# Gate, branch and output projections of a hybrid encoder block with the tokens stationary, and transposes behind them

## The chip, the cores and the metric

The kernel runs on one core of one Trainium2 chip. The metric is the device time of one execution in microseconds (us), the median of several runs; lower is better. The core's engines are TensorE (PE for its matmuls, PEld for its weight loads), VectorE (DVE), ScalarE (ACT), GpSimd (POOL) and SyncE (SP), which here issues most DMAs.

## The reference

One encoder layer over 256 tokens of width 2048, in float32. What matters here is the part between the input projection and the gated MLP:

```python
proj = jnp.einsum('bld,de->ble', rms_norm(x, g_mix[layer]), w_in[layer])   # 10240 columns
q, k, v, hy, gates = jnp.split(proj, splits, axis=-1)                       # gates: 2 x 2048
a_branch = jnp.einsum('ble,ed->bld', att.reshape(b, l, V_COLS), w_attn_branch[layer])   # 1024 -> 2048
h_branch = jnp.einsum('blc,cd->bld', y_hy, w_hyena_branch[layer])                       # 1024 -> 2048
g_a, g_h = jnp.split(gates, 2, axis=-1)
merged = jax.nn.sigmoid(g_a) * a_branch + jax.nn.sigmoid(g_h) * h_branch
x = x + jnp.einsum('bld,de->ble', merged, w_out[layer])                                 # 2048 -> 2048
hf = rms_norm(x, g_ffn[layer])
up = dwconv3(jnp.einsum('bld,df->blf', hf, w_up[layer]), ...)                           # 2048 -> 11264
x = x + jnp.einsum('blf,fd->bld', jax.nn.silu(gate_u) * val_u, w_down[layer])           # 5632 -> 2048
return rms_norm(x, g_final)
```

## The kernel before, in words

All weights are streamed once, in **chunks** of 128x1024 numbers (512 KB): two row blocks (k-tiles) of 128 rows by 512 columns. A chunk is loaded into `wr` (five buffers), and split into a high part `wh` (ACT cast) and a low part `wl` (DVE subtraction), three buffers each, so that two fp32r operands stand for one float32. Activations are split in the same way: an operand tile holds, for each k-tile, 256 columns of the high part and 256 of the low part, side by side. The product of the two low parts is left out.

A **group** is 512 output columns of one weight matrix, over all its k-tiles. `add_group` puts the group's chunks into one list; the main loop goes over that list (`for i in range(n)`, line 891): it issues the load of chunk i+5, the split of chunk i+2 and the matmuls of chunk i, then takes one finished step of an earlier group (`flush(1)`) and some of the background work (`run_bg`: filter, long convolution, attention heads). The framework's scheduler then sets each engine's order from that; an engine runs its own instructions strictly in that order. The groups come as hyena projections (6), gate h (4, `w_in` 16 to 19), v (2), branch h (4, `w_hb`), q and k (4), gate a (4, `w_in` 12 to 15), branch a (4, `w_ab`), output (4, `w_out`), up (22, `w_up`) and down.

`emit_mm` knows two forms for one k-tile:

- **channel-major** (`toks=None`): weights stationary. For each of four blocks of 128 output channels, one matmul of `wh` with 512 moving columns (both parts of the 256 tokens) and one of `wl` with 256. That is 8 matmuls and 4 x 768 = 3072 moving columns a k-tile, a *pair* for each block. The result lies with channels on partitions, in four PSUM banks, each with two halves that still have to be added (`merged_sum`: ACT copies one half, DVE adds the other).
- **token-major** (`toks=(0, 1)`): tokens stationary, the weight moving. For each of two blocks of 128 tokens, three matmuls of 512 moving columns (x high with `wh`, x high with `wl`, x low with `wh`). That is 6 matmuls and 2 x 3 x 512 = 3072 moving columns a k-tile, a *triple* for each block. The result lies with tokens on partitions, in two banks, and is complete.

Before the change, v and down are token-major, and everything else is channel-major. A gate's step (4 a group) is `merged_sum`, a multiplication by `rstd` and a sigmoid; for gate a the sigmoids are kept back (`gate_gen`) until attention has ended. Branch a's step merges both branches and splits the sum into `mg`, the operand of the output projection. The output projection's step adds the residual `x2T` (reloaded from `xT` in DRAM by `reload_x`), writes the scaled split of the sum into `xg`, the operand of up, and sums the squares for the norm; after the last group `norm` makes `rstd` from a matmul with ones (`rs2_ps`). Since down wants the residual with tokens on partitions, `x2tok_gen` then transposes `x2T` on TensorE, 8 times 4 transposes into `xt_ps`, among the first chunks of up.

Of the kernel before, what the change touches and what calls it, by code (L numbers as in the profile page):

```python
# [11 lines left out]
F32 = mybir.dt.float32  # L12
# [34 lines left out]
def block(ctx: ExitStack, tc: tile.TileContext, a, out):  # L47
# [20 lines left out]
    def add(o, x, y):  # L68
        tt(o, x, y, ALU.add)
# [4 lines left out]
    def mul(o, x, y):  # L74
        tt(o, x, y, ALU.mult)
# [10 lines left out]
    def act(o, x, f, **kw):  # L86
        nc.scalar.activation(out=o, in_=x, func=f, **kw)  # L87
# [99 lines left out]
    def merged_sum(pt, name):  # L187
        lo = etile("lo", f"lo_{name}")
        nc.scalar.copy(out=lo, in_=pt[:, T:])  # L189
        s = etile("sum", f"s_{name}")  # L190
        add(s, pt[:, :T], lo)
        return s
# [54 lines left out]
    def xop(kk):  # L247
        return xg[kk // 4][:, kk % 4, :]

    # ------------------------------------------------------------------ hyena  # L250
    hy = {}

    def hy_groups():
# [173 lines left out]
                split(yhy[ct // 4][:, ct % 4, :T], yhy[ct // 4][:, ct % 4, T:], z)  # L427
                yield

    # ------------------------------------------------------------------ gates and branches  # L430
    mix = {}

    def gate_h_groups():
        def step(g, c):
            def f(pts):
                if g == 0 and c == 0:
                    mix["h"] = [s8(f"mh{i}", [P, 8, T]) for i in range(2)]
                ct = g * 4 + c
                s = merged_sum(pts[c], f"gh{ct}")
                mul(s, s, rstd)  # L440
                act(mix["h"][ct // 8][:, ct % 8, :], s, AF.Sigmoid)
            return f
        for g in range(4):
            add_group(a["w_in"][16 + g], KT, 512, xop, [step(g, c) for c in range(4)])

    def branch_h_groups():
        def step(g, c):
            def f(pts):
                ct = g * 4 + c
                s = merged_sum(pts[c], f"bh{ct}")  # L450
                m = mix["h"][ct // 8][:, ct % 8, :]
                mul(m, m, s)
            return f
        for g in range(4):
            add_group(a["w_hb"][g], 8, 512, lambda kk: hy["y"][kk // 4][:, kk % 4, :],
                      [step(g, c) for c in range(4)])

    def gate_a_group(g):
        def step(c):
            def f(pts):  # L460
                if g % 2 == 0 and c == 0:
                    mix["ga", g // 2] = s8(f"ga{g // 2}", [P, 8, T])
# [4 lines left out]
        add_group(a["w_in"][12 + g], KT, 512, xop, [step(c) for c in range(4)])  # L467

    def gate_gen():
        for t in range(16):  # L470
            o = mix["ga", t // 8][:, t % 8, :]
            with tc.issue_after(at["end"]):
                act(o, o, AF.Sigmoid)
            if t % 4 == 3:
                yield

    def branch_a_group(g):
        def step(c):
            def f(pts):
                if g == 0 and c == 0:  # L480
                    mix["m"] = [s8(f"mg{i}", [P, 4, 512], F32R) for i in range(4)]
                ct = g * 4 + c
# [6 lines left out]
        add_group(a["w_ab"][g], 8, 512, lambda kk: at["o"][kk // 4][:, kk % 4, :], [step(c) for c in range(4)])  # L489

    # ------------------------------------------------------------------ attention
    at = {}

    def v_groups():
# [168 lines left out]
            stt(dst[:, h % 4, T:], pt[:, :T], at["gs"], hi.bitcast(F32), ALU.mult, ALU.subtract)  # L663
        yield

    # ------------------------------------------------------------------ output projection and FFN
    ff = {}

    def reload_x():
        ff["x2T"] = [s8(f"x2T{i}", [P, 8, T]) for i in range(2)]  # L670
        for i in range(2):
            nc.sync.dma_start(out=ff["x2T"][i], in_=a["xT"][8 * i:8 * i + 8].rearrange("k p t -> p k t"))

    def out_groups():
        def step(g, c):
            def f(pts):
                ct = g * 4 + c
                s = merged_sum(pts[c], f"wo{ct}")
                x2 = ff["x2T"][ct // 8][:, ct % 8, :]
                add(x2, x2, s)  # L680
                split_scaled(x2, ct, C_GFFN)
                sq = etile("cv", f"sq2{ct}")
                act(sq, x2, AF.Square)
                acc = sqacc[:, 0, :]
                if ct == 0:
                    nc.vector.tensor_copy(out=acc, in_=sq)
                else:
# [9 lines left out]
        def nop(pts):  # L697
            pass
        for g in range(4):
            add_group(a["w_out"][g], KT, 512, lambda kk: mix["m"][kk // 4][:, kk % 4, :],  # L700
                      [step(g, c) for c in range(4)] + ([nop, norm] if g == 3 else []))

    def x2tok_gen():
        ff["x"] = [s8(f"x2tok{t}", [P, D]) for t in range(2)]
        for t in range(2):
            for k4 in range(4):
                pt = bank(f"xt_ps{t}{k4}")
                for c in range(4):
                    kk = k4 * 4 + c
                    nc.tensor.transpose(out=pt[:, c * P:(c + 1) * P],  # L710
                                        in_=ff["x2T"][kk // 8][:, kk % 8, t * P:(t + 1) * P], identity=ident)
                nc.scalar.copy(out=ff["x"][t][:, k4 * 512:(k4 + 1) * 512], in_=pt)
                yield

    def up_groups():
        ff["m"] = {}
# [249 lines left out]

def _host(inp):
    i = {k: np.asarray(v) for k, v in inp.items()}
    r = dict(_consts())
    r["xT"] = i["x"][0].T.reshape(KT, P, T)  # L970
    order = []
    for g in range(4):
        order += [g, 4 + g]
# [53 lines left out]
```

## Time and profile before

| | |
|---|---|
| time, median of 3 runs (lowest to highest) | 1455.68 us (1455.35 to 1455.88) |
| span of the profiled execution | 1453.7 us |
| TensorE matmuls: busy, share of the span, count | 1440.7 us, 99%, 8068 |
| VectorE: busy, share | 1039.8 us, 72% |
| ScalarE: busy, share | 807.8 us, 56% |
| DMA, mean busy share of the 16 engines in 40 slices of the span | 0.3 to 0.7 |

The span runs from the first to the last instruction; the 2.0 us that the median is longer lie around it. A busy time is the union of the durations of an engine's instructions. Matmuls follow each other before the one ahead has ended, so the durations printed (0.39 us for 512 columns) overlap, and what a matmul costs is read from the distance between two starts.

### The profile page before, as it was taken

How to read it: one execution, taken by the hardware profiler on the slowest of the kernel's cores; microseconds unless marked ns; L12 is line 12 of the kernel's file. 1: busy time of each engine (PE TensorE's matmuls, PEld its weight loads, DVE VectorE, ACT ScalarE, POOL GpSimd, SP SyncE). 2: the span in 40 equal slices, each digit the busy share in tenths (PEclk: the TensorE clock that was granted, in tenths of full speed). 3: DMA queues.
4: the chain of work that ended last, by engine and by line, in shares of the span. 5: the costliest groups of instructions: out<-in, count | busy, mean ns of one | idle time of the engine just before them, and what ended most of it. 6: DMA issues, size and time to landing. Idle time of an engine off the chain costs nothing.

```text
span 1453.7 us, 21399 instructions
## 1 busy us (share of the span) xinstructions
PE 1440.7 (99%) x8068; PEld 1245.2 (86%) x8068; DVE 1039.8 (72%) x1697; ACT 807.8 (56%) x1274; POOL 13.0 (1%) x17
## 2 busy tenths in 40 slices
PE   8999999999999999999999999999999999999997
PEld 7888888888888888888888888888888888888897
DVE  7988887856677777967776786777877776545464
ACT  7655554544566656656665565555655555434353
POOL 3000000000000000000000000000000000000000
PEclk9999999999999999999999999999999999999999
DMA  7754444465544445565545555555555556555573
GB/s 274 246 174 160 164 170 170 152 234 185 175 159 146 151 144 185 197 237 190 188 171 189 182 184 188 188 189 188 181 186 187 185 189 219 196 193 192 197 253 126
DMA packets 79663, 271.96 MB, mean 187 GB/s; under 512 B 8959, under 2 KB 14112, under 8 KB 79304
## 3 DMA queue, kind: packets, MB, share of 16 engines
q1 hardware_dynamic: 78840, 269.54, 53.9%
q8 instruction: 63, 1.03, 0.3%
q10 hardware_dynamic: 720, 1.07, 0.2%
q14 instruction: 40, 0.33, 0.1%
HBM read 268.45 MB, written 2.11 MB: 186 GB/s over the span
## 4 chain that ended last, share of the span: by engine, by line
PE 97%; DVE 1%; DMA 1%; ACT 1%; issue 0%; SPq 0%; ACTq 0%; DVEq 0%
PE acc L90 93%; PE s_ps L90 1%; DMA wr<-in_w_in_dram 1%; DVE wl L66 1%; PE o_ps L90 0%; PE h_ps L90 0%; PE k_ps L90 0%; PE y_ps L90 0%; ACT wh L99 0%; PE wt_ps L611 0%; PE xt_ps L710 0%; PE ua_ps L90 0%; PE ub_ps L90 0%; DVE xg L78 0%; PE f_ps L90 0%
## 5 line engine op out<-in xcount | busy, mean ns | idle before, releaser
L90 PE MATMUL acc<-xg,wh 128*128 128x512 f32 x2560 | 908.5, 400 | 0.6 <-ACT sq L87 0.3
L66 DVE TENSOR_TENSOR wl<-wr,wh 128x1024 fp32r<-128x1024 f32 (+1 forms) x495 | 601.1, 1215 | 355.7 <-ACT wh L99 354.3
L99 ACT CAST wh<-wr 128x1024 fp32r<-128x1024 f32 (+1 forms) x495 | 516.4, 1043 | 525.7 <-PE acc L90 470.0
L90 PE MATMUL acc<-xg,wl 128*128 128x256 f32 x2560 | 716.1, 281 | 2.5 <-DVE wl L66 2.4
L90 PEld LDWEIGHTS acc<-xg,wh 128*128 128x128 f32 x2560 | 480.7, 188 | 118.6 <-issue 0.7
L90 PEld LDWEIGHTS acc<-xg,wl 128*128 128x128 f32 x2560 | 483.1, 189 | 6.1 <-DVE wl L66 4.7
L90 PE MATMUL acc<-wh,m 128*128 128x512 f32 (+1 forms) x832 | 218.2, 350 | 0.0
L90 PEld LDWEIGHTS acc<-wh,m 128*128 128x128 f32 x832 | 146.9, 189 | 20.6
L90 PE MATMUL acc<-wl,m 128*128 128x512 f32 (+1 forms) x416 | 145.7, 350 | 0.0
L90 PE MATMUL acc<-mg,wh 128*128 128x512 f32 x256 | 88.8, 391 | 0.0
L90 PEld LDWEIGHTS acc<-wl,m 128*128 128x128 f32 x416 | 78.7, 189 | 10.4 <-DVE wl L66 0.2
L90 PE MATMUL acc<-mg,wl 128*128 128x256 f32 x256 | 71.7, 280 | 0.0
L90 PEld LDWEIGHTS acc<-mg,wh 128*128 128x128 f32 x256 | 47.9, 187 | 10.5
L90 PEld LDWEIGHTS acc<-mg,wl 128*128 128x128 f32 x256 | 48.4, 189 | 0.0
L90 PE MATMUL acc<-yhy,wh 128*128 128x512 f32 x128 | 45.3, 399 | 0.0
L90 PE MATMUL acc<-att,wh 128*128 128x512 f32 x128 | 44.5, 392 | 0.0
L90 PE MATMUL acc<-wh,xg 128*128 128x512 f32 x128 | 40.5, 392 | 0.0
L78 DVE SCALAR_TENSOR_TENSOR sg<-s_up,pk,sg 128x255 f32<-128x255 f32 x88 | 39.4, 478 | 0.7
L78 DVE SCALAR_TENSOR_TENSOR vv<-s_up,pk,vv 128x255 f32<-128x255 f32 x88 | 39.3, 478 | 0.4
L189 ACT COPY lo_up<-acc 128x256 f32<-128x256 f32 x88 | 32.2, 366 | 11.5 <-PE acc L90 11.3
L90 PE MATMUL acc<-yhy,wl 128*128 128x256 f32 x128 | 35.9, 281 | 0.0
L90 PE MATMUL acc<-att,wl 128*128 128x256 f32 x128 | 35.8, 280 | 0.0
(198 smaller groups left out, 1070.8 us busy)
## 6 DMA issues: line engine op xcount, KB each, us to landing
wr<-in_w_up_dram SPq DMA_DIRECT2D x176, 512.0 KB, 3.2
wr<-in_w_in_dram SPq DMA_DIRECT2D x156, 512.0 KB, 3.3
wr<-in_w_down_dram SPq DMA_DIRECT2D x66, 512.0 KB, 3.3
wr<-in_w_out_dram SPq DMA_DIRECT2D x32, 512.0 KB, 3.3
wr<-in_w_down_t_dram SPq DMA_DIRECT2D x28, 512.0 KB, 3.9
wr<-in_w_hb_dram SPq DMA_DIRECT2D x16, 512.0 KB, 4.3
wr<-in_w_ab_dram SPq DMA_DIRECT2D x16, 512.0 KB, 3.3
wr<-in_w_in_dram SPq DMA_DIRECT2D x8, 256.0 KB, 4.4
```

The source lines that it names most:

```text
L66: nc.vector.tensor_tensor(out=o, in0=x, in1=y, op=op)
L78: nc.vector.scalar_tensor_tensor(out=o, in0=x, scalar=s, in1=y, op0=op0, op1=op1)
L90: nc.tensor.matmul(o, lhsT=lhsT, rhs=rhs, start=start, stop=stop)
L99: nc.scalar.copy(out=hi, in_=x)
L189: nc.scalar.copy(out=lo, in_=pt[:, T:])
```

## The change

- Gate h, branch h, gate a, branch a and the output projection go from channel-major to token-major (`toks=(0, 1)`); each group has two steps of 512 columns instead of four of 256, and no `merged_sum`. Gates are scaled by `rstd_tok`, a per-partition scale of the activation.
- Branch a's merged sum lies in `ga` with tokens on partitions; two further steps a group (`turn_step`) transpose it, 4 transposes a step, and split it into `mg`. The output projection does the same: the residual sum `xtok` is transposed 4 blocks a step, and `split_scaled` writes `xg` from PSUM.
- The residual `x` is loaded token-major, at the start of branch a, not at the start of the output projection; it stays in place until the end, and `x2tok_gen` is gone.
- The norm after the output projection is worked out per token (two values a partition), put on a diagonal and spread over partitions by one matmul of the same shape as before.

```diff
     def gate_h_groups():
-                s = merged_sum(pts[c], f"gh{ct}")
-                mul(s, s, rstd)
-                act(mix["h"][ct // 8][:, ct % 8, :], s, AF.Sigmoid)
+                act(mix["h"][t][:, g * 512:(g + 1) * 512], pts[t], AF.Sigmoid, scale=rstd_tok[:, t:t + 1])
-            add_group(a["w_in"][16 + g], KT, 512, xop, [step(g, c) for c in range(4)])
+            add_group(a["w_in"][16 + g], KT, 512, xop, [step(g, t) for t in range(2)], toks=(0, 1))
...
     def branch_h_groups():
-                s = merged_sum(pts[c], f"bh{ct}")
-                m = mix["h"][ct // 8][:, ct % 8, :]
-                mul(m, m, s)
+                m = mix["h"][t][:, g * 512:(g + 1) * 512]
+                mul(m, pts[t], m)
...
     def gate_a_group(g):
-                s = merged_sum(pts[c], f"ga{g}{c}")
-                o = mix["ga", g // 2][:, (g % 2) * 4 + c, :]
-                mul(o, s, rstd)
+                act(mix["ga"][t][:, g * 512:(g + 1) * 512], pts[t], AF.Copy, scale=rstd_tok[:, t:t + 1])
...
+    def to_channels(src, g, half, name):
+        pt = bank(name)
+        for j in range(2):
+            ct = g * 4 + half * 2 + j
+            for t in range(2):
+                nc.tensor.transpose(out=pt[:, j * T + t * P:j * T + (t + 1) * P],
+                                    in_=src[t][:, ct * P:(ct + 1) * P], identity=ident)
+        return pt
...
     def branch_a_group(g):
-                s = merged_sum(pts[c], f"ba{ct}")
-                mul(s, s, mix["ga", g // 2][:, (g % 2) * 4 + c, :])
-                add(s, s, mix["h"][ct // 8][:, ct % 8, :])
-                dst = mix["m"][ct // 4]
-                split(dst[:, ct % 4, :T], dst[:, ct % 4, T:], s)
+                o = mix["ga"][t][:, cs]
+                mul(o, pts[t], o)
+                add(o, o, mix["h"][t][:, cs])
+        def turn_step(half):
+            def f(pts):
+                pt = to_channels(mix["ga"], g, half, f"mt{g}{half}").rearrange("p (c t) -> p c t", c=2)
+                dst = mix["m"][g][:, half * 2:half * 2 + 2, :]
+                split(dst[:, :, :T], dst[:, :, T:], pt)
+            return f
+                  [step(0), step(1), turn_step(0), turn_step(1)], toks=(0, 1))
...
-    def reload_x():
-            nc.sync.dma_start(out=ff["x2T"][i], in_=a["xT"][8 * i:8 * i + 8].rearrange("k p t -> p k t"))
+    def load_x():
+            nc.sync.dma_start(out=ff["x"][t], in_=a["x"][t * P:(t + 1) * P, :])
     def out_groups():
-                s = merged_sum(pts[c], f"wo{ct}")
-                add(x2, x2, s)
-                split_scaled(x2, ct, C_GFFN)
-                act(sq, x2, AF.Square)
-                    add(acc, acc, sq)
+                add(x2, pts[t], x2)
+                act(sq, x2, AF.Square, accum_out=ss2[:, t, g:g + 1])
+        def turn_step(g, half):
+            def f(pts):
+                pt = to_channels(ff["x"], g, half, f"xt{g}{half}")
+                for j in range(2):
+                    split_scaled(pt[:, j * T:(j + 1) * T], g * 4 + half * 2 + j, C_GFFN)
+            return f
         def norm(pts):
-            mm(pt[:, :T], ones, sqacc[:, 0, :], True, True)
-            rsqrt_chain(rstd, pt[:, :T], T, "x2")
-            bg.append(x2tok_gen())
+            nc.vector.tensor_reduce(out=ms, in_=ss2, axis=AX.X, op=ALU.add)
...
+            for t in range(2):
+                ts(d[:, t * P:(t + 1) * P], ident, r2[:, t, 2:3], None, ALU.mult)
+            mm(pt[:, :T], ones, d, True, True)
+            nc.scalar.copy(out=rstd, in_=pt[:, :T])
-                      [step(g, c) for c in range(4)] + ([nop, norm] if g == 3 else []))
+                      [step(g, 0), step(g, 1), turn_step(g, 0), turn_step(g, 1)] + ([norm] if g == 3 else []),
+                      toks=(0, 1))
-    def x2tok_gen():
...
-    before(lambda: (drain(), setp(False, 1.0), bg.append(gate_gen())))
+    before(lambda: (drain(), setp(False, 1.0), bg.append(gate_gen()), load_x()))
-    before(reload_x)
```

Where the instructions stand. First TensorE at the start of the output projection, before the change (`acc196_0` to `_3` are the four banks of the group that starts with chunk 196, `mg0` its operand, `wh196` and `wl196` the chunk's parts):

```order
L90 MATMUL acc196_0_6245<-mg0_5827,wh196_6153 128x512
L90 MATMUL acc196_0_6245<-mg0_5827,wl196_6154 128x256
L90 MATMUL acc196_0_6245<-mg0_5827,wh196_6153 128x512
L90 MATMUL acc196_0_6245<-mg0_5827,wl196_6154 128x256
L90 MATMUL acc196_1_6246<-mg0_5827,wh196_6153 128x512
L90 MATMUL acc196_1_6246<-mg0_5827,wl196_6154 128x256
```

The same place after the change:

```order
L90 MATMUL acc196_0_5519<-wh196_5470,mg0_5231 128x512
L90 MATMUL acc196_0_5519<-wl196_5471,mg0_5231 128x512
L90 MATMUL acc196_0_5519<-wh196_5470,mg0_5231 128x512 x2
L90 MATMUL acc196_0_5519<-wl196_5471,mg0_5231 128x512
L90 MATMUL acc196_0_5519<-wh196_5470,mg0_5231 128x512
L90 MATMUL acc196_1_5520<-wh196_5470,mg0_5231 128x512
```

Pairs of 512 and 256 moving columns became triples of 512; two banks are written, not four.

TensorE in branch a after the change (`mt00` is the bank of the first transposes of group 0, `ga0` and `ga1` the merged sums of the two token blocks, `acc184` the next group, `wh185` that group's second chunk):

```order
L90 MATMUL acc184_1_5244<-wl185_5214,att0_4912 128x512
L90 MATMUL acc184_1_5244<-wh185_5213,att0_4912 128x512
L476 MATMUL mt00_5277<-ident_74,ga0_4475 128x128
L476 MATMUL mt00_5277<-ident_74,ga1_4476 128x128
L476 MATMUL mt00_5277<-ident_74,ga0_4475 128x128
L476 MATMUL mt00_5277<-ident_74,ga1_4476 128x128
L90 MATMUL acc184_0_5243<-wh186_5239,att1_4913 128x512
L90 MATMUL acc184_0_5243<-wl186_5240,att1_4913 128x512
```

The transposes of a group stand behind both token blocks of the next group's first two chunks (24 matmuls), and the other half of them one chunk later. DVE at that place after the change (`acc180` is group 0's result, `mh` the other branch):

```order
L66 TENSOR_TENSOR wl185_5214<-wr185_5149,wh185_5213 128x1024
L66 TENSOR_TENSOR ga0_4475<-acc180_0_5155,ga0_4475 128x512
L66 TENSOR_TENSOR ga1_4476<-acc180_1_5156,ga1_4476 128x512
L66 TENSOR_TENSOR ga0_4475<-ga0_4475,mh0_1883 128x512
L66 TENSOR_TENSOR wl186_5240<-wr186_5171,wh186_5239 128x1024
L66 TENSOR_TENSOR ga1_4476<-ga1_4476,mh1_1884 128x512
L66 TENSOR_TENSOR wl187_5262<-wr187_5191,wh187_5261 128x1024
L66 TENSOR_TENSOR wl188_5287<-wr188_5211,wh188_5286 128x1024
L66 TENSOR_TENSOR mg0_5231<-mt00_5277,mg0_5231 128x2x256
```

Four operations of 512 columns, with one weight split among them, stand ahead of what `mt00` reads; four steps of four operations of 256 columns stood there before.

TensorE in the first group of up, before the change (`rs2_ps` is the norm's matmul, `xt_ps00` the first of eight fours of transposes, `acc228` the group):

```order
L90 MATMUL acc228_3_7098<-xg2_79,wh232_7159 128x512
L90 MATMUL acc228_3_7098<-xg2_79,wl232_7160 128x256
L90 MATMUL rs2_ps_7233<-sqacc_81,ones_73 128x256
L710 MATMUL xt_ps00_7245<-ident_74,x2T0_6235 128x128 x4
L90 MATMUL acc228_0_7095<-xg2_79,wh233_7192 128x512
```

and after it:

```order
L90 MATMUL acc228_3_6197<-xg1_78,wh231_6219 128x512
L90 MATMUL acc228_3_6197<-xg1_78,wl231_6220 128x256
L90 MATMUL acc228_3_6197<-xg1_78,wh231_6219 128x512
L90 MATMUL acc228_3_6197<-xg1_78,wl231_6220 128x256
L90 MATMUL rs2_ps_6312<-rdiag_6309,ones_73 128x256
L90 MATMUL acc228_0_6194<-xg2_79,wh232_6250 128x512
L90 MATMUL acc228_0_6194<-xg2_79,wl232_6251 128x256
```

The norm's matmul, one chunk earlier than before, is now the last thing that stands between the pairs of up (the output projection's last transposes stand one chunk ahead of it); before, eight fours of transposes followed it, one a chunk.

## Rows read from the trace of the kernel before

**Rows 1.** The page: busy us (share) xinstructions; granted clock by slice; the chain by engine.

```profile
PE 1440.7 (99%) x8068; PEld 1245.2 (86%) x8068; DVE 1039.8 (72%) x1697; ACT 807.8 (56%) x1274; POOL 13.0 (1%) x17
...
PEclk9999999999999999999999999999999999999999
...
PE 97%; DVE 1%; DMA 1%; ACT 1%; issue 0%; SPq 0%; ACTq 0%; DVEq 0%
```

**Rows 2.** What TensorE waited for: us in total, times, longest us.

```profile
PE acc L90 <- DVE wl L66: 2.4, 3, 1.0
...
PE ua_ps L90 <- DVE uq L66: 0.3, 1, 0.3
```

**Rows 3.** TensorE by stretch: us, busy (matmuls, edge ones too), clock, DMA share, GB/s.

```profile
158.68:260.42 101.74, 101.74 (x614) 1.00 0.49 167
...
292.87:309.32 16.45, 16.45 (x73) 1.00 0.83 286
309.32:354.53 45.21, 45.21 (x257) 1.00 0.57 187
...
460.34:567.64 107.30, 107.30 (x610) 1.00 0.45 157
567.64:612.11 44.47, 44.47 (x260) 1.00 0.54 189
612.11:700.86 88.75, 88.75 (x515) 1.00 0.61 214
...
738.33:1201.98 463.65, 463.65 (x2627) 1.00 0.54 186
```

**Rows 4.** Token-major matmuls of v in order of time: start us, us.

```profile
301.62 0.61 PE L90 MATMUL acc<-wh,xg 128*128 128x512 f32 x2
302.07 0.39 PE L90 MATMUL acc<-wl,xg 128*128 128x512 f32 x1
302.30 0.61 PE L90 MATMUL acc<-wh,xg 128*128 128x512 f32 x2
...
304.34 0.61 PE L90 MATMUL acc<-wh,xg 128*128 128x512 f32 x2
```

**Rows 5.** Channel-major pairs after the first norm's matmul, in order of time.

```profile
33.42 0.59 PE L90 MATMUL rs_ps<-sqacc,ones 128*128 128x256 f32 x2
33.67 0.58 PE L90 MATMUL acc<-xg,wh 128*128 128x512 f32 x1
34.09 0.28 PE L90 MATMUL acc<-xg,wl 128*128 128x256 f32 x1
...
34.43 0.28 PE L90 MATMUL acc<-xg,wl 128*128 128x256 f32 x1
...
34.78 0.28 PE L90 MATMUL acc<-xg,wl 128*128 128x256 f32 x1
```

**Rows 6.** Two of the eight fours of transposes, with the matmul behind, in time order.

```profile
715.15 0.60 PE L710 MATMUL xt_ps<-ident,x2T 128*128 128x128 f32 x4
715.51 0.48 PE L90 MATMUL acc<-xg,wh 128*128 128x512 f32 x1
...
718.42 0.60 PE L710 MATMUL xt_ps<-ident,x2T 128*128 128x128 f32 x4
```

**Rows 7.** Channel-major pairs after the last transposes, in order of time.

```profile
739.11 0.40 PE L90 MATMUL acc<-xg,wh 128*128 128x512 f32 x1
...
741.23 0.40 PE L90 MATMUL acc<-xg,wh 128*128 128x512 f32 x1
```

**Rows 8.** Groups of DVE instructions by shape: count | busy us, mean ns | idle before.

```profile
L66 DVE TENSOR_TENSOR wl<-wr,wh 128x1024 fp32r<-128x1024 f32 x487 | 594.9, 1222 | 353.5 <-ACT wh L99 352.1
...
L66 DVE TENSOR_TENSOR x2tok<-x2tok,gb 128x512 f32<-128x512 f32 x6 | 3.9, 684 | 0.0
L66 DVE TENSOR_TENSOR x2tok<-acc,x2tok 128x512 f32<-128x512 f32 x6 | 3.8, 681 | 0.0
```

**Rows 9.** The tile of the reloaded residual: its two DMAs' issue, and us to landing.

```profile
L672 SPq DMA_DIRECT2D x2T<-in_xT_dram x2: 576/901/1226, 612.2 to 613.5; - x2
...
DMA to landing us min/median/max: 8.3/9.2/10.0
```

More of the change, by code (lines that the diff above doesn't have):

```diff
@@ L433, in gate_h_groups, with step @@
     def gate_h_groups():
-        def step(g, c):
+        def step(g, t):
             def f(pts):
-                if g == 0 and c == 0:
-                    mix["h"] = [s8(f"mh{i}", [P, 8, T]) for i in range(2)]
-                ct = g * 4 + c
-                s = merged_sum(pts[c], f"gh{ct}")
-                mul(s, s, rstd)
-                act(mix["h"][ct // 8][:, ct % 8, :], s, AF.Sigmoid)
+                if g == 0 and t == 0:
+                    mix["h"] = [s8(f"mh{i}", [P, D]) for i in range(2)]
+                act(mix["h"][t][:, g * 512:(g + 1) * 512], pts[t], AF.Sigmoid, scale=rstd_tok[:, t:t + 1])
             return f
         for g in range(4):
-            add_group(a["w_in"][16 + g], KT, 512, xop, [step(g, c) for c in range(4)])
+            add_group(a["w_in"][16 + g], KT, 512, xop, [step(g, t) for t in range(2)], toks=(0, 1))
     def branch_h_groups():
-        def step(g, c):
+        def step(g, t):
             def f(pts):
-                ct = g * 4 + c
-                s = merged_sum(pts[c], f"bh{ct}")
-                m = mix["h"][ct // 8][:, ct % 8, :]
-                mul(m, m, s)
+                m = mix["h"][t][:, g * 512:(g + 1) * 512]
+                mul(m, pts[t], m)
             return f
@@ L455, in branch_h_groups, with step @@
             add_group(a["w_hb"][g], 8, 512, lambda kk: hy["y"][kk // 4][:, kk % 4, :],
-                      [step(g, c) for c in range(4)])
+                      [step(g, t) for t in range(2)], toks=(0, 1))
     def gate_a_group(g):
-        def step(c):
+        def step(t):
             def f(pts):
-                if g % 2 == 0 and c == 0:
-                    mix["ga", g // 2] = s8(f"ga{g // 2}", [P, 8, T])
-                s = merged_sum(pts[c], f"ga{g}{c}")
-                o = mix["ga", g // 2][:, (g % 2) * 4 + c, :]
-                mul(o, s, rstd)
+                if g == 0 and t == 0:
+                    mix["ga"] = [s8(f"ga{i}", [P, D]) for i in range(2)]
+                act(mix["ga"][t][:, g * 512:(g + 1) * 512], pts[t], AF.Copy, scale=rstd_tok[:, t:t + 1])
@@ L466, in step @@
             return f
-        add_group(a["w_in"][12 + g], KT, 512, xop, [step(c) for c in range(4)])
+        add_group(a["w_in"][12 + g], KT, 512, xop, [step(t) for t in range(2)], toks=(0, 1))
     def gate_gen():
[L470 to L475, printed above, removed]
+        for g in range(4):
+            for t in range(2):
+                o = mix["ga"][t][:, g * 512:(g + 1) * 512]
+                with tc.issue_after(at["end"]):
+                    act(o, o, AF.Sigmoid)
+            yield
@@ L477, in branch_a_group, with step @@
+    def to_channels(src, g, half, name):
[6 more added lines that the diff above has]
+        return pt
     def branch_a_group(g):
-        def step(c):
+        def step(t):
             def f(pts):
-                if g == 0 and c == 0:
+                if g == 0 and t == 0:
@@ L481, in f @@
                     mix["m"] = [s8(f"mg{i}", [P, 4, 512], F32R) for i in range(4)]
-                ct = g * 4 + c
-                s = merged_sum(pts[c], f"ba{ct}")
-                mul(s, s, mix["ga", g // 2][:, (g % 2) * 4 + c, :])
-                add(s, s, mix["h"][ct // 8][:, ct % 8, :])
-                dst = mix["m"][ct // 4]
-                split(dst[:, ct % 4, :T], dst[:, ct % 4, T:], s)
-            return f
-        add_group(a["w_ab"][g], 8, 512, lambda kk: at["o"][kk // 4][:, kk % 4, :], [step(c) for c in range(4)])
+                cs = slice(g * 512, (g + 1) * 512)
@@ L667, in block, with step @@
     ff = {}
-    def reload_x():
-        ff["x2T"] = [s8(f"x2T{i}", [P, 8, T]) for i in range(2)]
-        for i in range(2):
-            nc.sync.dma_start(out=ff["x2T"][i], in_=a["xT"][8 * i:8 * i + 8].rearrange("k p t -> p k t"))
+    def load_x():
+        ff["x"] = [s8(f"xtok{t}", [P, D]) for t in range(2)]
+        for t in range(2):
+            nc.sync.dma_start(out=ff["x"][t], in_=a["x"][t * P:(t + 1) * P, :])
     def out_groups():
-        def step(g, c):
+        ss2 = cp.tile([P, 2, 4], F32, name="ss2")
+        r2 = cp.tile([P, 2, 4], F32, name="r2")
+        def step(g, t):
@@ L676, in f @@
             def f(pts):
-                ct = g * 4 + c
-                s = merged_sum(pts[c], f"wo{ct}")
-                x2 = ff["x2T"][ct // 8][:, ct % 8, :]
-                add(x2, x2, s)
-                split_scaled(x2, ct, C_GFFN)
-                sq = etile("cv", f"sq2{ct}")
-                act(sq, x2, AF.Square)
[L684 to L687, printed above, removed]
-                    add(acc, acc, sq)
+                x2 = ff["x"][t][:, g * 512:(g + 1) * 512]
@@ L693, in norm @@
-            mm(pt[:, :T], ones, sqacc[:, 0, :], True, True)
-            rsqrt_chain(rstd, pt[:, :T], T, "x2")
-            bg.append(x2tok_gen())
-        def nop(pts):
-            pass
+            ms, y, r = (r2[:, :, c] for c in range(3))
+            nc.vector.tensor_reduce(out=ms, in_=ss2, axis=AX.X, op=ALU.add)
+            ts(ms, ms, 1.0 / D, EPS, ALU.mult, ALU.add)
+            act(y, ms, AF.Sqrt)
+            nc.vector.reciprocal(out=r, in_=y)
+            mul(y, r, r)
+            mul(y, y, ms)
@@ L699, in out_groups @@
+            ts(y, y, -0.5, 1.5, ALU.mult, ALU.add)
+            mul(r, r, y)
+            d = etile("cv", "rdiag")
+            for t in range(2):
+                ts(d[:, t * P:(t + 1) * P], ident, r2[:, t, 2:3], None, ALU.mult)
+            pt = bank("rs2_ps")
+            mm(pt[:, :T], ones, d, True, True)
+            nc.scalar.copy(out=rstd, in_=pt[:, :T])
         for g in range(4):
             add_group(a["w_out"][g], KT, 512, lambda kk: mix["m"][kk // 4][:, kk % 4, :],
-                      [step(g, c) for c in range(4)] + ([nop, norm] if g == 3 else []))
@@ L703, in x2tok_gen @@
-    def x2tok_gen():
[L704 to L713, printed above, removed]
+                      [step(g, 0), step(g, 1), turn_step(g, 0), turn_step(g, 1)] + ([norm] if g == 3 else []),
@@ L970, in _host @@
     r["xT"] = i["x"][0].T.reshape(KT, P, T)
+    r["x"] = i["x"][0]
     order = []
```

2 lines of the change are left out of this document (added).

## Prediction

> **What bounds the kernel now.** I read the page first. TensorE's matmuls are busy for 1440.7 of 1453.7 us, the chain that ended last is 97% TensorE, and the granted clock is 0.9 or more in every slice [rows 1]. Next, what TensorE waited for: some three microseconds in all, 2.4 of them for weight parts [rows 2]. So the end is set by the number of matmuls and by the distance from one start to the next. VectorE and ScalarE have room, and what the change takes from them (the half sums, the scalings by `rstd`) is worth nothing by itself.
>
> Then the distances, since the printed durations overlap. The window view gives them by stretch. The output projection is 512 matmuls, 256 pairs, with nothing between them: 88.75 us, 0.3467 us a pair. The long stretch of up is 2624 matmuls, 1312 pairs, again with nothing between: 463.65 us, 0.3534 us a pair [rows 3] (the view counts two or three more at the edges). So the same pair has **two spacings**, a fast and a slow one 0.0067 us longer; the time order shows both: 34.09 to 34.78 is two pairs in 0.69 us [rows 5], 739.11 to 741.23 six pairs in 2.12 [rows 7]. Branch a goes at 44.47 / 128 = 0.347, branch h at 45.21 / 128 = 0.353 [rows 3].
>
> The token-major form is in this trace already: in v, from the same `xg` that the gates read, four triples take 301.62 to 304.34, 0.680 us each [rows 4]; the last 24 triples of v, with a restart at their head, 16.45 us, 0.685 each [rows 3]. Two pairs and one triple move the same 1536 columns: 0.693 or 0.707 us against 0.680. That difference is the change's gain.
>
> **The change part by part.** A k-tile is four pairs before and two triples after. Gate h, gate a and the output projection have 64 k-tiles each (256 pairs, 128 triples), the two branches 32 each (128 pairs, 64 triples). 128 triples are 87.0 us, 64 are 43.5.
>
> Branch h: 45.21 less 43.5, **1.7 us** saved. Branch a: 44.47 less 43.5, **0.95**. Output projection: 88.75 less 87.0, **1.7** [rows 3].
>
> Gate h shares its stretch with the convolution's matmuls: 101.74 us, 614 matmuls, 102 of them not the gate's [rows 3]. At the slow spacing the gate is 90.5 us, and 11.2 us are left for the others, 0.11 each, which is what a transpose takes (below); at the fast one 88.75, and 0.13 each. I take the slow one, **3.4 us** saved; the fast one gives 1.7. Gate a lies among attention's matmuls, 107.30 us [rows 3], where the rest doesn't tell the spacing: between 1.7 and 3.4, and I take the middle, **2.6**. Together 10.4 us.
>
> Transposes: 16 fours are added (8 in branch a, 8 in the output projection), and the 8 fours of `x2T` in up go. From one four to the next with eight pairs between is 718.42 - 715.15 = 3.27 us [rows 6]; less eight slow pairs (2.83) that is 0.44 us a four, and it includes the matmul behind, which takes 0.48 us, not 0.40. At fast pairs it would be 0.50. So 16 x 0.44 - 8 x 0.44 = **3.5 us** added; the upper end is 4.0.
>
> The norm keeps one matmul of the same shape; its chain works on two values a partition, and its result is due only at the end of up's first group, four chunks later: nothing. The residual's load moves from the output projection to the start of branch a and stays 2 MB. On SP's queue branch a's weight loads now stand behind it, and where it stood the output projection's did; it took 8.3 to 10.0 us to land [rows 9], and TensorE was busy for all 88.75 us of that stretch [rows 3]. Its buffers were last read by transposes of heads 6 and 7, several chunks back, so it holds nothing up. Its first use is 16 chunks later. I cost it at nothing; were the lead of some two chunks (8 triples, 5.4 us) all there is, it would be 4.6 us, once.
>
> New waits: TensorE, strictly in order, now has transposes that read what VectorE has just written. Ahead of `mt00`'s operand VectorE has four operations of 512 columns at 0.68 us and one weight split of 1.22 [rows 8], 3.95 us from the end of the group. TensorE meanwhile has 24 matmuls, 8 triples, 5.4 us. One more split ahead (5.2 us) would still fit. In the output projection two additions (1.4 us) stand there. Cost nothing.
>
> Sum: -10.4 + 3.5 = **-6.9 us**. The span goes from 1453.7 to 1446.8, and with the 2.0 us around it the median goes to **1448.8 us**. The weakest sum has both gates at 1.7, every triple at 0.685 (512 triples, 2.6 us dearer) and 4.0 for the transposes: 7.8 - 2.6 - 4.0 = 1.2 us saved. The best: 11.2 - 3.5 = 7.7.
>
> A note speaks against this. The rows say that two pairs cost 0.013 to 0.027 us more than one triple of as many columns, for one matmul more [rows 3, 4]. The Trainium skill, page "TensorE: Matmul & The Clock Gate", section "Back-to-back issue gap", puts the fixed part of a warm matmul at about 2.5 ns. By it the 512 matmuls that fall away would give an estimated 1.3 us, less than the transposes take, and the time would be 1457.9. The trace disagrees with it in this stream of load and matmul, by five times and more.
>
> **The rivals.** *Up goes over to the fast spacing.* A stream keeps its spacing until something is put between (the output projection ran on from branch a at the fast one [rows 3]), and what is put between can switch it: fast before the transposes, slow behind them [rows 5 to 7]. Now the last thing before 1376 pairs of up is the norm's matmul, and behind its twin at 33.42 the pairs went at the fast spacing [rows 5]; but they had done so ahead of it as well, and here it comes behind transposes. If it leaves up fast: 1376 x 0.0067 = 9.2 us more, 1439.6 us. Nearly an even chance; I leave up slow, as eight fours of transposes in a row left it.
>
> *The spacing belongs to the columns and the neighbours, not to the form.* If each column costs what it does in the pairs around, a triple takes 0.693 to 0.707 us in the changed groups, the gain is zero, and the transposes are left: +3.5 us, 1459.2, slower. It decides from a triple of 0.680 + 6.9 / 512 = 0.693 us on. Against it: v's triples have the same operand and weight stream and went at 0.680 [rows 4].
>
> *The transposes wait for VectorE.* If two more splits get ahead, the four starts 3.95 + 2.44 - 5.4 = 1.0 us late, before each of the 8 groups' first four; the gain is gone from 6.9 / 8 = 0.9 us of wait on. With a third split ahead, 2.2 us each: 8 x 2.2 - 6.9 = +10.7, 1466.4. For it: each group hands VectorE its work in two large pieces at once; against it: VectorE is busy for 72% [rows 1].
>
> **How the numbers follow.** The sum as it stands, up slow: 0.47. Up fast: 0.37. Columns alone count, or nearly: 0.06, split evenly between a loss and no change. Transposes or loads wait: 0.10, half of which leaves a loss. Forecast 1448.8. The range reaches from the fast case with the best sum (1453.7 - 7.7 - 9.2 + 2.0 = 1438.8) to the slow case with half of the gain lost to small waits (1452), and leaves out both losing rivals. Measuring this kernel tells apart about 0.2%, 2.9 us: faster 0.85, same 0.08, slower 0.07.
>
> **What would show it.** After the change: 8068 - 512 + 32 = 7588 matmuls; branch h near 43.5 us; branch a near 43.5 + 6 x 0.44 = 46.2 and the output projection near 87.0 + 8 x 0.44 = 90.5 (the last two fours of each stand in the next stretch); up with two fours, and its long stretch at 0.353 or 0.347 a pair, which decides between the first two cases. TensorE's wait on `ga` or `xtok` in the waiting view would show the third rival, triples of 0.70 us in the gates the second. I would be wrong altogether if TensorE's busy share fell, that is, if something other than the matmul starts set the end.

## The result, and the profile after

The changed kernel takes 1440.66 us (median of 4 runs, 1440.41 to 1440.69) against 1455.68. The ratio is 0.9896, with a 95% interval of 0.9882 to 0.991: **15.0 us faster**. The time lies in the predicted range, near its lower end; the gain is a little over twice the 6.9 us of the forecast, and close to the rival *up goes over to the fast spacing* (1439.6).

The profiled execution has a span of 1438.9 us. The page answers to [rows 1]: 480 matmuls fewer, as counted ahead, TensorE still busy 99% of the span, VectorE and ScalarE lighter, the granted clock at 9 in every slice.

```profile
PE 1426.2 (99%) x7588; PEld 1217.9 (85%) x7588; DVE 992.4 (69%) x1532; ACT 782.1 (54%) x1171; POOL 12.6 (1%) x17
...
PEclk9999999999999999999999999999999999999999
...
PE 98%; DVE 1%; ACT 1%; issue 0%; DMA 0%; SPq 0%; DVEq 0%
```

The whole answer on TensorE's waits, to be read against [rows 2] (us in total, times, longest). It adds up to 3.7 us, against 4.1 before:

```profile
PE acc L90 <- DVE wl L66: 2.1, 3, 0.8
PE warm L90 <- DVE ones L880: 1.1, 1, 1.1
PE ua_ps L90 <- DVE uq L66: 0.3, 1, 0.3
PE acc L90 <- ACT wh L99: 0.2, 1, 0.2
```

No line names `ga` or `xtok`: the new transposes never wait for VectorE, and the earlier load of the residual holds nothing up. So all of the gain must be in the distances between matmuls. The windows of after, by stretch, as in [rows 3] (us, busy and matmuls, clock, DMA share, GB/s): gate h, branch h, q and k, gate a, branch a, output, all of up, and up's last 1280 pairs.

```profile
158.29:257.14 98.85, 98.85 (x486) 1.00 0.55 171
306.06:349.58 43.52, 43.52 (x193) 1.00 0.63 193
349.58:455.39 105.81, 105.81 (x593) 1.00 0.53 161
455.39:560.21 104.82, 104.82 (x483) 1.00 0.52 165
560.21:606.72 46.51, 46.51 (x220) 1.00 0.65 215
606.72:697.61 90.89, 90.89 (x417) 1.00 0.59 185
697.61:1187.23 489.62, 489.62 (x2827) 1.00 0.61 189
743.50:1187.23 443.73, 443.73 (x2562) 1.00 0.62 190
```

The same last 1280 pairs of the kernel before:

```profile
749.71:1201.98 452.27, 452.27 (x2562) 1.00 0.54 186
```

Against the stretches before: gate h -2.9, branch h -1.7, gate a -2.5, branch a +2.0, output +2.1, and up 501.12 to 489.62, that is **-11.5**. The five stretches whose code was changed give 3.0 us together. The rest comes from up, whose pairs were not touched: 452.27 / 1280 is 353.3 ns a pair before, 443.73 / 1280 is 346.7 after.

Where the spacing turns is seen in the time order around the norm's matmul (start us, us):

```profile
708.72 0.40 PE L90 MATMUL acc<-xg,wh 128*128 128x512 f32 x1
...
709.08 0.40 PE L90 MATMUL acc<-xg,wh 128*128 128x512 f32 x1
...
709.43 0.40 PE L90 MATMUL acc<-xg,wh 128*128 128x512 f32 x1
709.66 0.28 PE L90 MATMUL acc<-xg,wl 128*128 128x256 f32 x1
709.78 0.59 PE L90 MATMUL rs_ps<-rdiag,ones 128*128 128x256 f32 x2
710.02 0.58 PE L90 MATMUL acc<-xg,wh 128*128 128x512 f32 x1
710.44 0.28 PE L90 MATMUL acc<-xg,wl 128*128 128x256 f32 x1
710.56 0.40 PE L90 MATMUL acc<-xg,wh 128*128 128x512 f32 x1
...
710.91 0.39 PE L90 MATMUL acc<-xg,wh 128*128 128x512 f32 x1
...
711.25 0.40 PE L90 MATMUL acc<-xg,wh 128*128 128x512 f32 x1
```

The pairs ahead start 0.35 to 0.36 us apart (slow, as they had been since the first pairs of up, ahead of its two fours of transposes), those behind 0.34 to 0.35. From there on it stays so for 1376 pairs.

### The profile page after: what moved, and what is told of

Same layout as the page of the kernel before. It is cut to its first block, busy times and chain, and to the rows that moved or that the text cites. A ratio compares the mean times of both kernels' runs of the same rounds, so it can differ in the third digit from the quotient of the medians.

```text
span 1438.9 us, 20120 instructions
## 1 busy us (share of the span) xinstructions
PE 1426.2 (99%) x7588; PEld 1217.9 (85%) x7588; DVE 992.4 (69%) x1532; ACT 782.1 (54%) x1171; POOL 12.6 (1%) x17
## 4 chain that ended last, share of the span: by engine, by line
PE 98%; DVE 1%; ACT 1%; issue 0%; DMA 0%; SPq 0%; DVEq 0%
PE acc L90 93%; PE s_ps L90 1%; PE y_ps L90 0%; PE o_ps L90 0%; PE h_ps L90 0%; PE k_ps L90 0%; DVE wl L66 0%; DMA wr<-in_w_in_dram 0%; PE wt_ps L620 0%; PE xt L476 0%; PE mt L476 0%; PE ua_ps L90 0%; PE ub_ps L90 0%; ACT wh L99 0%; ACT xg L87 0%
## 5 line engine op out<-in xcount | busy, mean ns | idle before, releaser
L90 PE MATMUL acc<-xg,wh 128*128 128x512 f32 x2048 | 715.6, 396 | 0.5 <-ACT wh L99 0.2
L90 PE MATMUL acc<-xg,wl 128*128 128x256 f32 x2048 | 568.1, 279 | 2.3 <-DVE wl L66 2.1
L90 PEld LDWEIGHTS acc<-xg,wh 128*128 128x128 f32 x2048 | 384.5, 188 | 91.2 <-ACT wh L99 0.9
L90 PEld LDWEIGHTS acc<-xg,wl 128*128 128x128 f32 x2048 | 385.2, 188 | 6.2 <-DVE wl L66 4.7
L90 PE MATMUL acc<-wh,xg 128*128 128x512 f32 x640 | 205.5, 394 | 0.0
L90 PEld LDWEIGHTS acc<-wh,xg 128*128 128x128 f32 x640 | 120.3, 188 | 25.6 <-issue 0.9
L90 PE MATMUL acc<-wl,xg 128*128 128x512 f32 x320 | 124.9, 390 | 0.0
L90 PE MATMUL acc<-wh,mg 128*128 128x512 f32 x256 | 81.3, 393 | 0.0
L90 PEld LDWEIGHTS acc<-wl,xg 128*128 128x128 f32 x320 | 60.3, 188 | 11.3
L90 PE MATMUL acc<-wl,mg 128*128 128x512 f32 x128 | 49.9, 390 | 0.0
```

## Experiments

Two theories stood at the outset. **The last thing between**: transposes leave a stream of pairs slow and a norm-shaped matmul leaves it fast, whichever stands last. **The state of the stream**: what is put between can switch the spacing, but which way depends on where in its pattern the stream was, and not on the kind of thing alone. In either, up's spacing is apart from what the projections gain. "Norm-shaped" is a matmul of 256 float32 columns, as the norm's. In each kernel below, up's last 1280 pairs are the reading that tells the spacing: 443.7 us fast, 452.3 slow.

### A norm-shaped matmul behind before's last transposes

```diff
+        pt = bank("rs3_ps")
+        mm(pt[:, :T], ones, sqacc[:, 0, :], True, True)
+        yield
```

These lines stand at the end of `x2tok_gen` of the kernel before; the result is not used.

> The kernel before, with one further matmul of the norm's shape (float32, ones by 256 columns, result unused) behind the last of the eight fours of transposes in up. Nothing else is changed. If what stands last between the pairs sets up's spacing: the 1296 pairs behind it go from 0.3534 to 0.3467-0.3471 us, 8.2 to 8.7 us less, and the matmul costs 0.43: 1447.4 to 1448 us. If up went fast in the changed kernel for another reason (the projections ahead, the token-major residual, the freed VectorE): pairs stay at 0.3534, and the time is 1456.1.

Measured 1456.25 us against 1455.72, ratio 1.0006 (0.9997 to 1.0016): no change, and the half microsecond is the matmul's own. The window of up's last 1280 pairs in this kernel:

```profile
750.44:1202.71 452.27, 452.27 (x2562) 1.00 0.56 186
```

The added matmul in its time order; the trace shortens its bank's name to `rs_ps`:

```profile
741.18 0.40 PE L90 MATMUL acc<-xg,wh 128*128 128x512 f32 x1
741.42 0.28 PE L90 MATMUL acc<-xg,wl 128*128 128x256 f32 x1
741.53 0.59 PE L90 MATMUL rs_ps<-sqacc,ones 128*128 128x256 f32 x2
741.77 0.58 PE L90 MATMUL acc<-xg,wh 128*128 128x512 f32 x1
```

Up stayed slow behind the same kind of matmul that had made it fast in after. The first theory fell.

### Transposes behind after's norm

```diff
+        def turn_again(pts):
+            to_channels(ff["x"], 3, 1, "xt_again")
...
-                      ... ([norm] if g == 3 else []),
+                      ... ([norm, turn_again] if g == 3 else []),
```

> The changed kernel, with four further transposes (result unused) one chunk behind the norm's matmul in up. If what stands last sets the spacing: the 1368 pairs behind go back to 0.3534 us, 8.6 us more, and the four costs 0.44: 1449.7 us, near the 1448.8 that was forecast. If the spacing has another cause: pairs stay at 0.347, 1441.1 us.

Measured 1441.11 us, ratio 0.9899 (0.9885 to 0.9914). Up's last 1280 pairs:

```profile
744.32:1188.06 443.74, 443.74 (x2563) 1.00 0.62 190
```

Up stayed fast behind four transposes. The first theory fell from this side too.

### Twenty things put into before's up

One thing in the middle of each of 20 groups of up: fours and twos of transposes (t), norm-shaped matmuls (n), one or three fp32r matmuls of 512 columns (w), one of 256 (h), a float32 one of 64 (s).

```diff
+    kinds = ["t4", "n1", "t4", "n1", "t2", "t2", "t2", "w3", "w3", "w3", "w1", "w1", "n1", "h1", "h1", "t4", "h1", "s1", "t4", "s1"]
...
+        if i in probe:
+            between(probe[i], f"pr{i}")
```

> The kernel before, with twenty things put between the pairs of up, one in the middle of each group from the third on (results unused): in order four transposes, the norm's matmul, four, norm's, two transposes three times, three fp32r matmuls of 512 columns three times, one of 512 twice, norm's, one fp32r of 256 twice, four transposes, one of 256, a norm-shaped matmul of 64 columns, four transposes, the 64-column one again. The spacing of the eight groups' pairs behind each is read from the trace. If the last thing between sets it: slow behind every four, fast behind every norm's matmul, whichever it was ahead; then the time is between 1446 and 1462. If the state ahead matters too, the same thing is followed by different spacings: two transposes and three matmuls would change over each time. If neither does: 0.3534 throughout.

One run: 1462.41 us. In no stretch between two things did the spacing change by itself, and the same kind was followed by either: norm-shaped by slow, fast, slow (787.8, 833.9, 1040.1 us); three fp32r matmuls by slow, fast, slow (925.0, 948.3, 971.1); twos of transposes by slow, also once where it had been fast (856.5). All three norm-shaped ones came behind slow pairs. The one at 833.9 in the time order, fast behind it:

```profile
833.86 0.59 PE L90 MATMUL pr<-sqacc,ones 128*128 128x256 f32 x2
834.10 0.58 PE L90 MATMUL acc<-xg,wh 128*128 128x512 f32 x1
...
834.64 0.40 PE L90 MATMUL acc<-xg,wh 128*128 128x512 f32 x1
...
835.68 0.39 PE L90 MATMUL acc<-xg,wh 128*128 128x512 f32 x1
```

The one at 1040.1 in the time order of the same kernel, slow behind it:

```profile
1040.11 0.59 PE L90 MATMUL pr<-sqacc,ones 128*128 128x256 f32 x2
1040.35 0.58 PE L90 MATMUL acc<-xg,wh 128*128 128x512 f32 x1
...
1040.89 0.40 PE L90 MATMUL acc<-xg,wh 128*128 128x512 f32 x1
...
1041.95 0.40 PE L90 MATMUL acc<-xg,wh 128*128 128x512 f32 x1
```

Three pairs take 835.68 - 834.64 = 1.04 us behind the first, 1041.95 - 1040.89 = 1.06 behind the second. The starts in nanoseconds show the pattern. Slow pairs come in a cycle of three: `wh` to `wl` and `wl` to the next `wh` are 241 and 120, 236 and 113, 233 and 117 ns. Fast pairs are either all 230 and 117 (steady), or 231 and 112 and 233 and 117 in turn (alternating). Behind the pair 241/119 the norm-shaped matmul left the stream fast (833.9), behind 236/116 slow (787.8 and 1040.1). That is the second theory in a form that can be tried: the place in the cycle decides.

### Before's added matmul, eight pairs on

The first experiment's matmul stood behind a pair of 236/116. One more `yield` ahead of it moves it by one chunk step, 8 pairs, to another place of the cycle of three.

```diff
+        yield
         pt = bank("rs3_ps")
         mm(pt[:, :T], ones, sqacc[:, 0, :], True, True)
         yield
```

> As e1 (the kernel before with a further norm-shaped matmul behind the transposes of up), but that matmul stands one chunk, 8 pairs, further on. In the slow spacing three pairs repeat (gaps of 240 and 120 ns, 236 and 113, 233 and 117); in the runs so far a norm-shaped matmul behind the 236/113 pair left the stream slow (four times of four), behind each of the other two it left it fast (four of four). In e1 it came behind 236/113. Eight pairs on is two places further in the cycle of three, so behind 240/120. If place in the cycle decides: 1288 pairs at 0.3467 instead of 0.3534 us, 8.6 less than e1: 1447.6 us. If it doesn't, as e1: 1456.2.

Measured 1447.50 us against 1455.68, ratio 0.9942 (0.9927 to 0.9957), as expected. Up's last 1280 pairs, in the kernel whose only difference from the kernel before is one unused matmul:

```profile
749.77:1193.50 443.73, 443.73 (x2562) 1.00 0.58 190
```

This is the cleanest evidence that up's spacing is a thing by itself: **8.2 us** without any of the change.

### After's norm, eight pairs on

```diff
-                      ... ([norm] if g == 3 else []),
+                      ... ([lambda pts: None, norm] if g == 3 else []),
```

> The changed kernel with the norm's step one chunk later, so that its matmul stands 8 pairs further on in up; nothing is added. In the changed kernel it came behind the 233/117 pair; two places further in the cycle is the 236/113 pair. If place in the cycle decides: up stays slow, 1368 pairs at 0.3534 instead of 0.3471 us, 8.6 us more: 1449.3 us, and the gain over the kernel before is 6.4, near the 6.9 that was forecast. If it doesn't: 1440.7.

Measured 1440.79 us, ratio 0.9893 (0.9877 to 0.991): a miss. The matmul came where it was meant to, behind a pair of 236/115, and up was fast all the same:

```profile
743.75:1187.48 443.73, 443.73 (x2563) 1.00 0.62 190
```

The first step of the pair behind it, from `wh` to `wl`, was 425 ns, not 417 to 421 as behind the other norm-shaped ones. So the place in the cycle goes far, but does not settle it alone.

### Norm-shaped matmuls and threes in turn

The same places in before's up, with the two kinds that had switched most often.

```diff
-    kinds = ["t4", "n1", "t4", ...]
+    kinds = ["n1", "w3"] * 10
```

> The kernel before with ten norm-shaped matmuls and ten threes of fp32r matmuls (results unused), in turn, between the pairs of up, one in the middle of each group from the third on. Asked: does the place in the slow cycle of three pairs settle what a norm-shaped matmul does? So far, behind the 236/113 pair it left the stream slow five times and fast once (the run with the norm one chunk on), behind the others fast each time. If place settles it: each one behind 236/113 stays slow here, each other goes fast. If it doesn't: mixed results behind the same pair. Threes between fast pairs: slow each time. Time between 1448 and 1464.

One run: 1462.83 us. The first norm-shaped one came behind a slow pair of 233/120 and left the stream fast; the second behind 236/116 and left it slow; the next eight, all behind the alternating fast form, left it slow every time. So the expected "each other goes fast" holds behind slow pairs only. The threes: from steady fast to slow once, from slow (the last pair 233/117 each time) to fast nine times of nine. All norm-shaped matmuls in the traces of all twelve kernels (before, after and the ten here) that have pairs on both sides:

| last pairs ahead | then fast | then slow |
|---|---|---|
| slow cycle, last pair 236/116 | 1 | 5 |
| slow cycle, last pair 233/120 or 241/119 | 11 | 0 |
| steady fast, 230/117 | 8 | 0 |
| alternating fast | 0 | 8 |

The norm in after is among the eleven (233/119 ahead). The prediction's only specimen, at 33.42 [rows 5], is among the eight behind steady fast pairs: it could tell nothing of a stream that comes in slow. (Ahead of this run the traces held four slow outcomes behind the 236 pair, not the five that the expectation counts.)

For threes the place settles it in every case on record. Each kernel has 16 threes of 512 columns among the first pairs, of the filter and its transform (`h_ps`, `k_ps`); with those put in, the twelve traces hold 206. Behind fast pairs they left the stream slow, 97 times of 97; behind a slow pair of 236/113 or 233/117 fast, 104 of 104; behind 241/120 slow, 5 of 5. In the kernel before, each of the 16 switched the spacing: the eight pairs ahead of the three at 92.43, then the eight behind it, are

```profile
89.62:92.43 2.81, 2.81 (x17) 1.00 0.48 175
93.13:95.90 2.77, 2.77 (x17) 1.00 0.39 157
```

### After with three matmuls behind the norm

```diff
+        def three(pts):
+            pt, op = bank("three"), xop(0)
+            for _ in range(3):
+                mm(pt, op[:, :P], op, True, True)
...
-                      ... ([norm] if g == 3 else []),
+                      ... ([norm, three] if g == 3 else []),
```

> The changed kernel with three fp32r matmuls of 512 columns (results unused) one chunk behind the norm's matmul in up. In every run so far that stood between fast pairs of this kind, such a three left them slow. If the switch is the cause of up's gain: 1368 pairs at 0.3534 instead of 0.3471 us, 8.6 more, and 0.7 for the three: 1450.0 us; without the three's own 0.7 that is 1449.3, against 1448.8 forecast. If up's gain has another cause: 1441.4.

Measured 1451.29 us against 1455.77, ratio 0.9969 (0.9956 to 0.9981). The three make up slow, and 10.6 us of the change's 15.0 are gone. Of the 11.0 us between the two profiled spans (1449.9 and 1438.9) 9.8 are in up, where the three themselves take 0.7, and 1.2 ahead of gate h, in the start. The windows of up and of its last 1280 pairs:

```profile
698.86:1198.27 499.41, 499.41 (x2830) 1.00 0.60 186
...
746.01:1198.27 452.26, 452.26 (x2562) 1.00 0.60 186
```

The three in this kernel's time order, and two pairs 0.36 us apart behind them:

```profile
714.24 0.85 PE L90 MATMUL three<-xg 128*128 128x512 f32 x3
714.93 0.40 PE L90 MATMUL acc<-xg,wh 128*128 128x512 f32 x1
...
715.97 0.40 PE L90 MATMUL acc<-xg,wh 128*128 128x512 f32 x1
...
716.33 0.40 PE L90 MATMUL acc<-xg,wh 128*128 128x512 f32 x1
```

With this there are four corners: before 1455.7 slow and 1447.5 fast, after 1451.3 slow and 1440.7 fast. At the same spacing of up the change gives 4.4 us slow and 6.8 us fast; without the added matmul (0.4, by the first experiment's up) and the three (0.7) it is 5.1 and 6.4, and the 5.1 has the start's 1.2 against it.

### The output projection alone

The kernel before with the change's `load_x`, output steps, transposes and norm; gates and branches stay channel-major.

```diff
-                      [step(g, c) for c in range(4)] + ([nop, norm] if g == 3 else []))
+                      [step(g, 0), step(g, 1), turn_step(g, 0), turn_step(g, 1)] + ([norm] if g == 3 else []),
+                      toks=(0, 1))
```

> Only the output projection, its transposes, the residual and the norm token-major; gates and branches as before. The output projection saves 1.7 us and takes six fours of transposes at 0.49; up loses six of its eight fours and two stay, 2.7 less. With up slow: 1455.7 - 1.7 + 2.9 - 2.7 = 1454.2. TensorE's order from the output projection on is that of the changed kernel, so by the place in the cycle up goes fast: another 8.8 less, 1445.4 us.

Measured 1445.79 us, ratio 0.9927 (0.9912 to 0.9941). Output, then up:

```profile
612.52:702.48 89.96, 89.96 (x411) 1.00 0.58 188
702.48:1192.09 489.61, 489.61 (x2827) 1.00 0.59 189
```

The output projection itself is 1.2 us *longer* than before [rows 3], since six of its eight fours lie in it; up gives 11.5. So this part of the change brings its 9.9 us almost wholly where none of its matmuls stand.

### Gates and branches alone

The changed kernel with before's output projection: `reload_x`, the channel-major steps and `x2tok_gen` are back.

```diff
-                      [step(g, 0), step(g, 1), turn_step(g, 0), turn_step(g, 1)] + ([norm] if g == 3 else []),
-                      toks=(0, 1))
+                      [step(g, c) for c in range(4)] + ([nop, norm] if g == 3 else []))
...
+    before(reload_x)
```

> Only the gates and branches token-major, with branch a's transposes; output projection, residual and norm as before. Saves 2.9 in gate h, 1.7 in branch h, 2.5 in gate a; branch a grows by 2.0; the two last fours of transposes fall in the output projection, 1.0. Up slow as before: 1455.7 - 4.1 = 1451.6 if the output projection's pairs stay fast, 1453.3 if they go slow behind the transposes. If the gain of 15 belonged to these projections: 1441.

Measured 1453.19 us, ratio 0.9983 (0.9973 to 0.9992). The number is that of the expectation's case with a slow output projection, but the windows (branch a, output, up) say otherwise:

```profile
559.97:608.57 48.60, 46.93 (x222) 1.00 0.57 182
608.57:698.08 89.51, 89.51 (x521) 1.00 0.65 206
698.08:1199.20 501.12, 501.12 (x2852) 1.00 0.59 185
```

The output's pairs are fast: 89.51 us, six late transposes among them. Branch a is 4.1 us longer than before, not 2.0 as in after: the event that calls `reload_x` first finishes all of branch a's open steps, so the last group's eight transposes come at once (the other 24 are spaced as in after). The first two of them end the stretch, and they wait for VectorE. The view of TensorE's waits in this kernel has the line:

```profile
PE mt L476 <- DVE ga L66: 1.7, 1, 1.7
```

That is the price of the third rival where it does come, once. The expectation's number was met by the wrong way. Up is slow, as before.

### After without the transposes of the merged branches

```diff
-                pt = to_channels(mix["ga"], g, half, f"mt{g}{half}").rearrange("p (c t) -> p c t", c=2)
+                pt = mix["ga"][half][:, g * 512:(g + 1) * 512].rearrange("p (c t) -> p c t", c=2)
```

> The changed kernel without the eight fours of transposes in branch a: mg is split from ga as it lies, so the output projection gets a wrongly arranged operand and the output isn't the reference's. If a four costs what the stretches of the changed kernel show (0.48 to 0.50 us): 3.9 us less, 1436.8 us. By the 0.44 of the forecast 3.5 less, 1437.2. If the transposes were hidden or TensorE waited for them: 0, or much more than 4.

Measured 1436.86 us, ratio 0.987 (0.9856 to 0.9885): 3.8 us less than after, 0.48 us for each of eight fours. Branch a falls from 46.51 to 43.63:

```profile
560.35:603.98 43.63, 43.63 (x196) 1.00 0.69 229
```

## Why the prediction was wrong

**The failed step** is the choice between two cases that the prediction had itself worked out: "I leave up slow, as eight fours of transposes in a row left it." Up went fast, and its own pairs dropped by the 9 us that the rival gave (8.54 us in the last 1280 pairs). The rival's price was right, and so was what it hung on; the reason for choosing against it was not. What the prediction had wrong is the last restart: it let a norm's matmul behind slow pairs leave them slow. Behind the 233 and 241 pairs of the slow cycle such a matmul left the stream fast eleven times of eleven, behind the 236 pair slow five times of six, and after's stood behind 233. "Transposes leave up slow" was a rule from one place in one trace. Fours behind slow pairs did leave them slow in all traces (101 of 101), but four behind after's fast pairs left them fast, and the trace of before had transposes that did otherwise: two that came behind slow pairs and had fast ones after them (555.24), and six between fast pairs (567.07), right ahead of branch a, which went at the fast spacing [rows 3].

```profile
555.24 0.38 PE L658 MATMUL ot_ps<-ident,osb 128*128 128x128 f32 x2
567.07 0.82 PE L658 MATMUL ot_ps<-ident,osb 128*128 128x128 f32 x6
```

The row at 33.42 was no better for the other side, and before's up has no norm's matmul with slow pairs ahead of it. The trace of before could have shown only that the matter was open, and the chances 0.47 and 0.37 said nearly that; the one number forecast could not.

**The matmul form**: right. Branch h 43.52 us for 192 matmuls, 226.7 ns each, 680 a triple, as read from v [rows 4]. Gate h gave 2.9 of an expected 3.4 and gate a 2.5 of 2.6; with gate h's triples at 680 ns, what stands between them takes an estimated 11.8 us (98.85 - 128 x 0.680), not the 11.2 that the prediction left for it. The rival *columns alone* is refuted: a triple of 693 ns would have made branch h 44.4. So is, for this stream, the estimate of 1.3 us for the matmuls that fall away, worked out from what the Trainium skill, page "TensorE: Matmul & The Clock Gate", section "Back-to-back issue gap", gives for a matmul by itself: at one and the same spacing of up the whole change gives 5 to 6 us, net of its transposes.

**The transposes**: mis-sized. A four in a stream of triples costs 0.48 to 0.50 us ((46.51 - 43.52) / 6 in branch a, 0.48 by the run without them), not the 0.44 that was read between slow pairs. Sixteen of them are 0.6 to 1.0 us dearer. Branch a came out at 46.5 for 46.2, output at 90.9 for 90.5.

**Hidden work**: right. VectorE, the norm's new chain and the residual's earlier load cost nothing; the waits of after show none of them. (The "some three microseconds" of waits that the prediction read for before leave out 1.1 us at the warm-up; all of them are 4.1.)

Together: the five changed stretches gave 3.0 us. Of up's 11.5, six fours fewer are some 2.7, and 8.8 is spacing. Projections and transposes alone are thus 5.7 us for a forecast of 6.9. Another 0.4 us lies ahead of gate h, which starts at 158.29 us, not at 158.68. From the first weight matmul to there it is 153.1 to 154.8 us in before, after and the kernels above that differ from them only in up, so it is not the change's.

**What stays open**: why such a stream has two spacings, and what decides at a restart. The runs of one kernel lie closer together than the 8 us between the two (after: 1440.41 to 1440.69; the widest, with the three: 1450.22 to 1453.28), so up's spacing is not chance from run to run. The first pairs are less firm: ahead of the first norm's matmul, at 33 us, where none of the edits reach, they came slow in four of the twelve traces and fast in eight. And what a restart does moves with shifts of a few nanoseconds in the restart, and the run with after's norm eight pairs on is an exception to the best description I have. Whether TensorE's weight loads or the matmuls themselves keep the cycle was not tried.

## What to carry to other kernels

Where TensorE is never idle, cost a change by the start-to-start distances in each stretch, and expect them to move in stretches that the change doesn't touch: here 8.8 of 15 us came from 1376 untouched pairs that restarted on another beat. Before such a gain is put down to an edit, run the kernels with the spacing turned each way; one unused matmul did it here. A precedent for what a restart does counts only if the stream came into it in the same state.

## What the runs showed of the chip that I had not expected

- A stream of pairs, 512 and 256 moving columns with a weight load each, has two stable spacings at the same granted clock: 346.7 ns in a steady or an alternating form, and 353.3 ns in a cycle of three pairs. It keeps either for over 450 us. One unused matmul of 256 float32 columns, put at the right pair, takes 8.2 us off this kernel; eight pairs earlier it takes nothing.
- A stream of 128x512 matmuls alone, each with its weight load, as in branch h after, went at 226.7 ns a matmul.
- Three matmuls of 512 columns between such pairs switched the spacing in the same way in all twelve traces: fast to slow 97 times of 97, slow to fast 104 times of 109, and the five left slow all stood behind the 241/120 pair.
- Four float32 transposes cost 0.44 us among slow pairs and 0.48 to 0.50 us among triples, the longer step of the matmul behind them included.
